# Layer 0 of a hybrid decoder trunk: the recurrent gate's projection as 512-wide products, and another order of work around the recurrence

## The chip, the cores and the metric

The kernel runs on one core of a Trainium2 chip. The metric is the device time of one execution in microseconds (us); below that stand profiled executions, in which the hardware recorded every instruction. The engines are named as in the profile: PE (TensorE, matrix products; PEld is its loading of stationary operands), DVE (VectorE), ACT (ScalarE), POOL (GpSimd) and SP (SyncE, which issues most DMAs).

## The reference

Two layers over x of 256 positions and width 1024, all in float32. Each layer normalizes x, projects it once into the inputs of three branches and their gates, and adds the projected, gated outputs to x:

```
proj = rms_norm(x) @ w_in        # a_q a_k a_v a_g | b_x b_g | c_q c_k c_v c_g
y_a = dilated_attention(a_q, a_k, a_v) * silu(a_g)      # 8 heads of 64
y_b = rg_lru(conv(b_x)) * silu(b_g)                     # width 256
y_c = stick_breaking_attention(c_q, c_k, c_v) * silu(c_g)   # 4 heads of 64
x = x + concat(y_a, y_b, y_c) @ w_out
```

The recurrent branch (b) is a linear recurrence h[t] = a[t] h[t-1] + u[t], with r and i two sigmoid gates of the convolved input xc, log a = 8 r log_sigmoid(lambda), and u = sqrt(1 - a^2) i xc. Its gate silu(b_g) multiplies h. A last normalization follows the two layers.

## The kernel before

**Precision.** PE multiplies in a reduced float32 format. So that nothing is lost, each weight and each activation is split into a rounded part (hi, made by ACT, line 115) and its rest (lo, made by DVE as the difference, line 117), and a product is the sum of hi*hi, hi*lo and lo*hi.

**Weights.** They come in chunks of 128 x 2048, two DMAs on SP each (line 108), into staging tiles st of which there are five. Each chunk is split in four parts of 512 columns, `rounds[l, c]` (ACT) and `rests[l, c]` (DVE), into tiles whi and wlo, of which there are four each; so chunk n + 4 can only be rounded when PE has read chunk n. In layer 0 the order of the chunks is CQ, CK, AQ0, AK0, BX, AQ1, AK1, CG, BG, AG, AG+1 and then four of the output projection, O to O+3 (called O1, O2, O3 here for O+1 to O+3). Chunk BG gives the recurrent gate, AG and AG+1 the gates of the attention heads, CG that of the stick-breaking heads. A chunk is requested one or two chunks ahead (`ask`).

**Projections** (`proj_b`, line 326). A chunk of 256 output columns is made in two halves of 128, with the weights stationary. There are two forms. A chunk that is not in PAIRED[l] takes 24 products of 256 columns a half, all into one PSUM bank for both halves (`mm3`, line 225): hi weights with the x's hi, hi weights with its lo, lo weights with its hi. A chunk in PAIRED[l] takes 8 products of 512 columns (line 344: hi weights with the x's hi and lo side by side) and 8 of 256 columns (line 341: lo weights with the x's hi) a half, into a bank of its own; first half hi weights first, second half lo weights first. ACT then copies the bank's right side into `low` (line 347), and DVE adds the left side to it (line 349). In layer 0 the result is still to be scaled by the row norms rb (`scaled`, line 415), since x goes in unnormalized there; then comes the sigmoid (line 439) and a multiplication (line 440).

**Order.** PE runs in the order of the program text (`manual_schedule`). The other engines' order is made when the program is built, by a list scheduler that takes what it reckons ready, earlier text first. `dep(a, b)` makes it place a behind b; in this diff both are always on one engine, so nothing is synchronized by it, and at run time each engine simply goes through its list.

**Around the change, layer 0.** PE's list is: CG; the transposes of the first four heads' probabilities; BG's first half; then `third()`: the recurrent gates (line 609), the values of the stick-breaking heads, those of the first four attention heads (line 458, into a bank of the pool pp), and the scores of the last four; BG's second half; AG; AG+1; and the output projection in the order of output tiles (t, n2) = (0,0), transposes of the last four heads, (1,0), (0,1), values of the last four heads, (1,1), each over the recurrent and stick-breaking part of y (chunks O and O1); then the attention part (O2, O3). The pool pp has three banks. The first attention values keep one from line 690 until `emit_y(y_c["y"], ...)`, line 715, has multiplied them (line 444); output tile (0,0) goes to another pool, the later ones to pp.

The recurrence (`lru_gates`, `lru_scan`) goes over ACT and DVE in turns: gates (ACT), `silu(bg)`: scaled (DVE), sigmoid (ACT), multiplication (DVE); a table load (line 78) on ACT, the decays av (line 623), a2 = av^2 (line 626, `last["a2"]`), the gap (a2 + 1) th (line 627), logarithm and exponential for its root (lines 628 and 629), products and the scan (lines 630 and 632), y = h * gate (line 444), its hi part (line 446) and its rest (line 447), which PE reads in output tile (0,0). In the same stretch runs the softmax of the last four heads (`dil_softmax`, line 560): eight exponentials (line 566, `last["exps"]`), four reciprocals (line 568, `last["recs"]`) and eight multiplications (line 570).

Of the kernel before, what the change touches and what calls it, by code (L numbers as in the profile page):

```python
# [12 lines left out]
AF = mybir.ActivationFunctionType  # L13
ALU = mybir.AluOpType
# [28 lines left out]

CH_AV, CH_CV, CH_CQ, CH_CK, CH_BX, CH_CG, CH_BG, CH_AG, CH_O = 0, 2, 3, 4, 7, 10, 11, 12, 14
CH_AQ, CH_AK = (5, 8), (6, 9)
PAIRED = ((CH_BX, CH_AQ[1], CH_AK[1], CH_CG, CH_AG, CH_AG + 1), (CH_CQ, CH_CK, CH_AQ[0], CH_AK[0], CH_BX, CH_AQ[1], CH_AK[1], CH_CG, CH_BG, CH_AG, CH_AG + 1))


@with_exitstack
def trunk_kernel(ctx: ExitStack, tc: tile.TileContext, x, first_x, first, wpack, prm_d, gatew, gains, consts, rope, out):  # L50
    nc = tc.nc
    act, dve, pe, gps = nc.scalar, nc.vector, nc.tensor, nc.gpsimd
# [10 lines left out]
    def bank(pool, tag):  # L63
        return pool.tile([P, 512], F32, name=tag, tag=tag)

    def scr(w):
        return wk.tile([P, 512], F32, name="scr", tag="scr", bufs=SCR)[:, 0:w]
# [3 lines left out]
    def dep(inst, on):  # L71
        tc.add_manual_dep(inst.ins, on.ins.name, nosync)
        return inst
# [9 lines left out]
    def tab(*a, **k):  # L83
        i = dep(act.activation(*a, **k), loaded["load"])  # L84
        loaded["users"].append(i)
        return i

    def v2(a, n=2):
        return a.rearrange("p (b t) -> p b t", b=n)
# [10 lines left out]
    split, rounds, rests = {}, {}, {}  # L100
# [23 lines left out]
    def ask(l, c, ahead=AHEAD):  # L124
        last = order.index((l, c)) + ahead
        while pending and order.index(pending[0]) <= last:
            i = pending.pop(0)
            ready[i] = load_chunk(*i)

    def weights(l, c, ahead=AHEAD):  # L130
        ask(l, c, ahead)
        return ready.pop((l, c))
# [87 lines left out]
    def mm3(ps, lhs, rhs, ks, first, last, skip=False):  # L220
        lh, ll = lhs
        rh, rl = rhs
        seq = [(a, b, k) for a, b in ((lh, rh), (lh, rl), (ll, rh)) for k in ks]
        for i, (a, b, k) in enumerate(seq):
            pe.matmul(ps, a(k), b(k), start=first and i == 0, stop=last and i == len(seq) - 1,  # L225
                      skip_group_check=skip)

    last = {}
# [82 lines left out]
    for l in range(L):  # L311
# [14 lines left out]
        def proj_b(c, mid=None, to=None, sc=1.0):  # L326
            pair = c in PAIRED[l]
            hi, lo = [a.rearrange("p (k c) -> p k c", c=256) for a in weights(l, c, AHEAD - 1 if mid else AHEAD)]
            if pair:
                flat = None if to is not None else scr(512)  # L330
                to = [v2(flat)[:, b, :] for b in range(2)] if to is None else to
            else:
                flat = bank(pp, "pp")
            for b in range(2):
                cs = slice(b * P, b * P + P)
                if pair:
                    ps = last["bank"] = bank(pp, "pp")
                    seq = [(b ^ i, k) for i in range(2) for k in range(NK)]
                    for i, (is_lo, k) in enumerate(seq):
                        if is_lo:  # L340
                            pe.matmul(ps[:, 0:S], lo[:, k, cs], xh[:, k, :], start=i == 0, stop=i == len(seq) - 1,  # L341
                                      skip_group_check=True)
                        else:
                            pe.matmul(ps, hi[:, k, cs], xx[:, k].rearrange("p h t -> p (h t)"), start=i == 0,  # L344
                                      stop=i == len(seq) - 1, skip_group_check=True)
                    low = wk.tile([P, S], F32, name="low", tag="low", bufs=2)
                    last["low"] = last["low", c, b] = act.activation(low, ps[:, S:2 * S], AF.Copy, scale=sc)  # L347
                    if sc == 1.0:
                        last["sum"] = last["sum", c, b] = dve.tensor_add(to[b], ps[:, 0:S], low)  # L349
                    else:  # L350
                        dve.scalar_tensor_tensor(to[b], ps[:, 0:S], sc, low, ALU.mult, ALU.add)
                else:
                    mm3(flat[:, b * 256:(b + 1) * 256], [lambda k, a=a: a[:, k, cs] for a in (hi, lo)],
                        [lambda k, a=a: a[:, k, :] for a in (xh, xl)], range(NK), b == 0, True, True)
                if b == 0 and mid:
                    mid()
                    ask(l, c)
            return flat

        def proj_to(dst, c, mid=None, sc=1.0):  # L360
            if c in PAIRED[l]:
                proj_b(c, mid, [dst[:, b, :] for b in range(2)], sc)
# [67 lines left out]
        def home(tile_):  # L430
            return [tile_[:, b, :] for b in range(2)] if l == 0 else None

        def silu(dst, ps):
            sg = v2(scr(512))
            src = dst if ps is None else v2(ps)
            if l == 0:
                ps, src = src, v2(scr(512))
                scaled(src, ps.rearrange("p b t -> p (b t)"))
            tab(sg, src, AF.Sigmoid)
            dve.tensor_mul(dst, src, sg)  # L440

        def emit_y(src, gate, k0, n):
            dst = v2(scr(n * S), n)
            dve.tensor_mul(dst, src, gate)
            yh, yl = [v[:, k0 % 4:k0 % 4 + n, :] for v in ys[k0 // 4]]
            act.activation(yh, dst, AF.Copy)
            last["rest", k0] = dve.tensor_sub(yl, dst, yh.bitcast(F32))

        def head(h):
# [58 lines left out]
        def rotated(c, tiles, h0, tag, mid=None):  # L508
            dst = tiles[h0] = sb.tile([P, 2, S], F32, name=tag, tag=tag)
            tab_ = rp0 if l == 0 else rp  # L510
            pair = c in PAIRED[l]
            if pair:
# [75 lines left out]
        th = sb.tile([P, 2, S], F32, name="th", tag="th")  # L588
        bg = sb.tile([P, 2, S], F32, name="bg", tag="bg")
# [29 lines left out]
        def lru_scan():  # L619
            av = sb.tile([P, 2, S], F32, name="av", tag="bxp")  # L620
            for b in range(2):
                o = 2 * l + b
                tab(av[:, b, :], rt[:, b, :], AF.Exp, scale=c8[:, o:o + 1])
            dve.tensor_mul(it, it, xc)
            a2 = v2(scr(512))
            last["a2"] = dve.tensor_mul(a2, av, av)
            dve.scalar_tensor_tensor(a2, a2, 1.0, th, ALU.add, ALU.mult)
            tab(th, a2, AF.Ln, bias=tiny)
            tab(th, th, AF.Exp, scale=0.5)
            dve.tensor_mul(it, it, th)  # L630
            for b in range(2):
                dve.tensor_tensor_scan(rt[:, b, :], av[:, b, :], it[:, b, :], 0.0, ALU.mult, ALU.add)
# [57 lines left out]
            y_c["y"] = values(va, pts, 0, bank(pp, "pp"))  # L690
            y_c["s"] = dil_scores(4)

        bg_ps = proj_b(CH_BG, third)
        if l == 0:
            for r in rests[l, CH_AG + 1]:
                dep(r, cg_scaled)
# [9 lines left out]
        ps = None  # L706
        if CH_AG in PAIRED[l]:
            agf = sb.tile([P, 2, S], F32, name="agf", tag="cg")
# [3 lines left out]
        ps = proj_b(CH_AG) if ps is None else ps  # L712
        table(SIGM)
        silu(ag[:, 0:2, :], ps)
        emit_y(y_c["y"], ag[:, 0:2, :], 4, 2)
        seeded = proj_b(CH_AG + 1)
        silu(ag[:, 2:4, :], seeded)
        if l == 0:
            for r in rests[l, CH_O][1:]:
                dep(r, bg_scaled)  # L720
            for r in rounds[l, CH_O + 1][2:]:
                dep(r, last["low", CH_AG, 0])
            dep(last["a2"], last["sum", CH_AG, 0])
            for r in rounds[l, CH_O][1:]:
                dep(r, last["gate"])
            for r in (*rests[l, CH_O][4:], *rests[l, CH_O + 1]):
                dep(r, last["sum", CH_AG, 0])
        if CH_AG + 1 in PAIRED[l]:
            seeded = last["bank"]
# [12 lines left out]
            act.activation(seed, xres[:, 1, 512 + LATE:1024], AF.Copy)  # L742
        for n2 in range(2):
            w = weights(l, CH_O + n2)
            for t in range(NT):
                if l > 0 and (t, n2) == (1, 1):
                    tail = [(bank(yp, "y")[:, 0:LATE], 0, LATE), (seed, LATE, 512)]
                    for ps, c0, c1 in tail[::-1]:
                        out_mm(ps, w, t, 0, range(4), c0 == 0, False, c0, c1, c0 > 0)
                    continue  # L750
                o_ps[t, n2] = bank(at, "s") if (t, n2) == (0, 0) else bank(pp, "pp")
                for ks in ((0, 1), (2, 3)):
                    out_mm(o_ps[t, n2], w, t, 0, ks, ks[0] == 0, False)
                if (t, n2) == (0, 0):
                    y_c["p"] = dil_transposes(4)
                if (t, n2) == (0, 1):
                    emit_y(values(va, y_c["p"], 4), ag[:, 2:4, :], 6, 2)
# [133 lines left out]
```

## Time and profile before

| | us |
|---|---|
| median of three runs | 245.64 |
| lowest, highest | 245.21, 245.93 |
| the profiled execution | 244.72 |
| its span, first to last instruction | 242.8 |
| PE, DVE, ACT busy in it | 236.1, 202.2, 177.2 |

Views of the profile give start and duration of instructions in us from the start of the span. Rows of the timeline can hold several instructions (x2); an engine's next instruction can start while the end of the last is still counted, so a step is best read from start to start. A bracket at the end is idle time of the engine, and what ended it. The chain of waits goes back from the last instruction to what released each one.

### The profile page before, as it was taken

The page shows a single profiled execution, that of the slowest core. Times are in us where ns is not written, and L with a number is a line of the kernel's source. Part 1 is how long each engine was busy: PE and PEld are TensorE (multiplying, and loading weights), DVE is VectorE, ACT ScalarE, POOL GpSimd, SP SyncE. Part 2 cuts the span into 40 slices and gives each one's busy share as a digit, 9 for nine tenths or more (in the row PEclk, how much of TensorE's full clock was granted, in tenths as well). Part 3 has the DMA queues.
Part 4 walks back from the last instruction along what each step waited for, and adds up shares of the span by engine and source line. Part 5 has one row for each costly group of instructions (what it writes and reads, how often), then busy time and mean ns, then how long its engine had stood idle before and what let it go on. Part 6 is the DMA issues. An engine that isn't in the chain of part 4 may idle for free.

```text
span 242.8 us, 4458 instructions
## 1 busy us (share of the span) xinstructions
PE 236.1 (97%) x1587; PEld 203.5 (84%) x1587; DVE 202.2 (83%) x488; ACT 177.2 (73%) x392; POOL 10.4 (4%) x43
## 2 busy tenths in 40 slices
PE   8999999999999999999999999999999999999991
PEld 4888999998888888778888888888888888887881
DVE  3885898999999989997793666999999986997362
ACT  3769977839958789994863775876579858997243
POOL 0017200002000000000000000000010000000000
PEclk9999999999999999999999999999999999999998
DMA  6999988455266753269457397505470772000022
GB/s 187 403 274 385 403 319 270 155 177 182 79 211 219 245 166 117 87 171 341 181 173 257 109 288 281 179 16 187 163 216 26 242 257 75 11 0 3 0 86 88
DMA packets 14037, 43.88 MB, mean 181 GB/s; under 512 B 1728, under 2 KB 3008, under 8 KB 14016
## 3 DMA queue, kind: packets, MB, share of 16 engines
q1 hardware_dynamic: 13248, 42.43, 51.9%
q0 software_dynamic: 192, 0.52, 0.9%
q10 hardware_dynamic: 576, 0.66, 0.8%
q8 instruction: 12, 0.20, 0.4%
q14 instruction: 9, 0.07, 0.1%
HBM read 42.03 MB, written 1.05 MB: 177 GB/s over the span
## 4 chain that ended last, share of the span: by engine, by line
PE 69%; DVE 24%; DMA 2%; ACT 2%; issue 1%; SPq 0%; DVEq 0%
PE pp L225 19%; PE pp L344 17%; PE pp L341 9%; PE s L225 8%; DVE wlo L117 7%; PE s L181 4%; PE pp L385 2%; PE s L494 2%; DMA st<-first 2%; PE pp L181 2%; PE y L458 2%; DVE scr L555 2%; DVE pr L570 2%; DVE sw L485 1%; PE y L225 1%; PE s L548 1%
## 5 line engine op out<-in xcount | busy, mean ns | idle before, releaser
L117 DVE TENSOR_TENSOR wlo<-st,whi 128x512 fp32r<-128x512 f32 x128 | 82.6, 688 | 7.1 <-ACT whi L115 6.5
L115 ACT ACTIVATE whi<-st 128x512 fp32r<-128x512 f32 x130 | 73.1, 628 | 11.3 <-DMA st<-w_pack 7.3
L344 PE MATMUL pp<-xx,whi 128*128 128x512 f32 x272 | 66.5, 393 | 0.0
L344 PEld LDWEIGHTS pp<-xx,whi 128*128 128x128 f32 x272 | 49.4, 188 | 9.7 <-DVE q L349 0.3
L341 PEld LDWEIGHTS pp<-xx,wlo 128*128 128x128 f32 x272 | 35.2, 191 | 2.1 <-ACT scr L84 0.3
L341 PE MATMUL pp<-xx,wlo 128*128 128x256 f32 x272 | 36.8, 285 | 0.0
L225 PE MATMUL pp<-xx,whi 128*128 128x256 f32 x160 | 21.1, 285 | 0.0
L225 PEld LDWEIGHTS pp<-xx,whi 128*128 128x128 f32 x160 | 19.8, 191 | 0.5 <-issue 0.3
L347 ACT ACTIVATE low<-pp 128x256 f32<-128x256 f32 x34 | 12.5, 373 | 10.4 <-PE pp L344 9.6
L78 ACT ACT_TABLE_LOAD x13 | 16.7, 1283 | 1.9 <-PEq L884 1.7
L84 ACT ACTIVATE pr<-scr,mn 128x128 f32<-128x128 f32 (+1 forms) x32 | 14.2, 446 | 3.9 <-DVE mn L555 3.9
L225 PE MATMUL pp<-whi,yh 128*128 128x512 f32 (+1 forms) x48 | 14.1, 382 | 0.0
L225 PE MATMUL pp<-wlo,yh 128*128 128x512 f32 (+1 forms) x48 | 13.6, 372 | 0.0
L225 PE MATMUL pp<-whi,yl 128*128 128x512 f32 (+1 forms) x48 | 13.6, 371 | 0.0
L225 PE MATMUL pp<-xx,wlo 128*128 128x256 f32 x80 | 11.2, 283 | 0.0
L225 PEld LDWEIGHTS pp<-xx,wlo 128*128 128x128 f32 x80 | 10.3, 192 | 0.0
L181 PE MATMUL s<-whi,xx 128*128 128x512 f32 (+1 forms) x36 | 10.1, 399 | 0.1
L225 PEld LDWEIGHTS pp<-whi,yl 128*128 128x128 f32 x48 | 8.6, 188 | 1.6
L225 PEld LDWEIGHTS pp<-wlo,yh 128*128 128x128 f32 x48 | 8.6, 188 | 1.6
L225 PEld LDWEIGHTS pp<-whi,yh 128*128 128x128 f32 x48 | 8.3, 188 | 1.6 <-issue 0.3
L555 DVE CUSTOM_DVE_ANT_0 scr<-s,con 128x128 f32<-128x128 f32 (+1 forms) x32 | 9.2, 353 | 0.0
L485 DVE TENSOR_TENSOR_SCAN sw<-scr,con 128x127 f32<-128x127 f32 (+1 forms) x16 | 8.0, 540 | 0.9 <-ACT scr L84 0.9
(193 smaller groups left out, 375.3 us busy)
## 6 DMA issues: line engine op xcount, KB each, us to landing
st<-w_pack SPq DMA_DIRECT2D x66, 512.0 KB, 4.8
st<-first SPq DMA_DIRECT2D x7, 512.0 KB, 5.9
xres<-x_in SPq DMA_DIRECT2D x4, 256.0 KB, 6.7
gw_t<-gate_w SPq DMA_DIRECT2D x2, 256.0 KB, 6.7
gn<-gains SPq DMA_DIRECT2D x2, 256.0 KB, 6.5
xs<-xc POOLq DMA_DIRECT2D x4, 128.0 KB, 3.3
gf<-gains SPq DMA_DIRECT2D x2, 256.0 KB, 6.1
out<-st ACTq DMA_DIRECT2D x2, 192.0 KB, 2.0
```

The source lines that it names most:

```text
L78: load = act.preload_act_table_set(name)
L84: i = dep(act.activation(*a, **k), loaded["load"])
L115: split[l, c] = act.activation(h, part, AF.Copy)
L117: rests.setdefault((l, c), []).append(dve.tensor_sub(r, part, h.bitcast(F32)))
L181: pe.matmul(ps[t][:, c0:c1], a[:, k, t * P:(t + 1) * P], b, start=k == 0 and all(m[0] is not ps for m in seq[:i]), stop=k == NK - 1 and al ...
L225: pe.matmul(ps, a(k), b(k), start=first and i == 0, stop=last and i == len(seq) - 1, skip_group_check=skip)
L341: pe.matmul(ps[:, 0:S], lo[:, k, cs], xh[:, k, :], start=i == 0, stop=i == len(seq) - 1, skip_group_check=True)
L344: pe.matmul(ps, hi[:, k, cs], xx[:, k].rearrange("p h t -> p (h t)"), start=i == 0, stop=i == len(seq) - 1, skip_group_check=True)
L347: last["low"] = last["low", c, b] = act.activation(low, ps[:, S:2 * S], AF.Copy, scale=sc)
L385: pe.matmul(cv_bk[t][:, 0:512 >> i], a[:, k, t * P:(t + 1) * P], cv_w[k // 4][:, k % 4, 0:2 - i].rearrange("p h c -> p (h c)"), start=i == ...
L485: dve.tensor_tensor_scan(w[:, lo:lo + n][:, ::-1], om[:, lo + 1:lo + 1 + n][:, ::-1], diag[:, 255 - n:255][:, ::-1], 0.0, ALU.mult, ALU.add)
L555: last["min"] = dve.tensor_tensor_reduce(xs[:, cs], sps[h][:, cs], nmask[:, cs], -0.125, 3e38, ALU.add, ALU.min, mn[:, t:t + 1])
```

## The change

Four things, all in layer 0:

1. BG joins PAIRED[0]: 16 products of 512 and 16 of 256 columns replace 48 of 256. Each half has its own bank, a copy (line 347) and a sum (line 349) into bg; the scaling by rb then reads bg.
2. Behind the gap step (line 627) are placed: the last rest of chunk O, all rests of O1, and the last three reciprocals of the softmax. Behind the root's exponential (line 629): the last four exponentials of the softmax.
3. Behind the sigmoid of the first attention gate (`ag_sig`): the last two roundings of O1 and all of O2. That sigmoid itself stands behind the hi part of the recurrent y (`last["high", 2]`).
4. Behind the multiplication of the first attention values (`last["y", 4]`, line 444): the last three rests of O1 and all of O2.

The rest of the diff records instructions under names.

```diff
-PAIRED = ((CH_BX, CH_AQ[1], CH_AK[1], CH_CG, CH_AG, CH_AG + 1), ...
+PAIRED = ((CH_BX, CH_AQ[1], CH_AK[1], CH_CG, CH_BG, CH_AG, CH_AG + 1), ...
...
-        bg_ps = proj_b(CH_BG, third)
+        bg_ps = proj_b(CH_BG, third, home(bg))
...
         silu(ag[:, 0:2, :], ps)
+        ag_sig = last["sig"]
...
             dep(last["a2"], last["sum", CH_AG, 0])
+            for r in (*rests[l, CH_O][3:], *rests[l, CH_O + 1], *last["recs"][1:]):
+                dep(r, last["gap"])
+            for r in last["exps"][4:]:
+                dep(r, last["root"])
+            for r in rounds[l, CH_O + 1][2:]:
+                dep(r, ag_sig)
+            for r in rests[l, CH_O + 1][1:]:
+                dep(r, last["y", 4])
+            dep(ag_sig, last["high", 2])
             for r in rounds[l, CH_O][1:]:
                 dep(r, last["gate"])
-            for r in (*rests[l, CH_O][4:], *rests[l, CH_O + 1]):
+            for r in (*rests[l, CH_O][3:], *rests[l, CH_O + 1]):
                 dep(r, last["sum", CH_AG, 0])
...
             w = weights(l, CH_O + n2)
+            if l == 0 and n2 == 0:
+                for r in rounds[l, CH_O + 2]:
+                    dep(r, ag_sig)
+                for r in rests[l, CH_O + 2]:
+                    dep(r, last["y", 4])
```

`home(bg)` gives the two halves of bg as targets in layer 0 and nothing in layer 1, where BG was in PAIRED already.

More of the change, by code (lines that the diff above doesn't have):

```diff
@@ L45 @@
 CH_AQ, CH_AK = (5, 8), (6, 9)
-PAIRED = ((CH_BX, CH_AQ[1], CH_AK[1], CH_CG, CH_AG, CH_AG + 1), (CH_CQ, CH_CK, CH_AQ[0], CH_AK[0], CH_BX, CH_AQ[1], CH_AK[1], CH_CG, CH_BG, CH_AG, CH_AG + 1))
+PAIRED = ((CH_BX, CH_AQ[1], CH_AK[1], CH_CG, CH_BG, CH_AG, CH_AG + 1), (CH_CQ, CH_CK, CH_AQ[0], CH_AK[0], CH_BX, CH_AQ[1], CH_AK[1], CH_CG, CH_BG, CH_AG, CH_AG + 1))
 @with_exitstack
@@ L438, in silu @@
                 scaled(src, ps.rearrange("p b t -> p (b t)"))
-            tab(sg, src, AF.Sigmoid)
+            last["sig"] = tab(sg, src, AF.Sigmoid)
             dve.tensor_mul(dst, src, sg)
@@ L443, in emit_y @@
             dst = v2(scr(n * S), n)
-            dve.tensor_mul(dst, src, gate)
+            last["y", k0] = dve.tensor_mul(dst, src, gate)
             yh, yl = [v[:, k0 % 4:k0 % 4 + n, :] for v in ys[k0 // 4]]
-            act.activation(yh, dst, AF.Copy)
+            last["high", k0] = act.activation(yh, dst, AF.Copy)
             last["rest", k0] = dve.tensor_sub(yl, dst, yh.bitcast(F32))
@@ L626, in lru_scan @@
             last["a2"] = dve.tensor_mul(a2, av, av)
-            dve.scalar_tensor_tensor(a2, a2, 1.0, th, ALU.add, ALU.mult)
+            last["gap"] = dve.scalar_tensor_tensor(a2, a2, 1.0, th, ALU.add, ALU.mult)
             tab(th, a2, AF.Ln, bias=tiny)
-            tab(th, th, AF.Exp, scale=0.5)
+            last["root"] = tab(th, th, AF.Exp, scale=0.5)
             dve.tensor_mul(it, it, th)
```

## The prediction

> **What bounds the kernel now.** I read the page first, then the waits of TensorE between 22 and 238 us, then its timeline around the change, and last the timelines of VectorE and ScalarE in the same stretch.
>
> ```profile
> span 242.8 us, 4458 instructions
> PE 236.1 (97%) x1587; PEld 203.5 (84%) x1587; DVE 202.2 (83%) x488; ACT 177.2 (73%) x392; POOL 10.4 (4%) x43
> ```
> ```profile
> PE s L225 <- DVE yl L447: 0.2, 1, 0.2
> ```
>
> The second fence is the whole answer for TensorE's waits: one, on line 447, the rest of the gated recurrence output. A busy PE is no proof that it is never held, so I looked at the starts of its matmuls.
>
> ```profile
> 81.92 2.17 PE L225 MATMUL pp<-xx,whi 128*128 128x256 f32 x16
> 83.93 1.12 PE L225 MATMUL pp<-xx,wlo 128*128 128x256 f32 x8
> 84.89 2.00 PE L344 MATMUL pp<-xx,whi 128*128 128x512 f32 x8
> ...
> 88.64 3.82 PE L344 MATMUL pp<-xx,whi 128*128 128x512 f32 x16
> 92.30 2.08 PE L341 MATMUL pp<-xx,wlo 128*128 128x256 f32 x16
> ...
> 97.86 0.61 PE L225 MATMUL s<-wlo,yh 128*128 128x512 f32 x2
> 98.65 0.73 PE L225 MATMUL s<-whi,yl 128*128 128x512 f32 x2 [0.17 <-DVE yl L447]
> 99.22 1.48 PE L494 MATMUL s<-con,pr 128*128 128x128 f32 x12
> 100.46 0.73 PE L225 MATMUL pp<-whi,yh 128*128 128x512 f32 x2
> ```
>
> From 81.92 to 97.86 one group starts where the former leaves off. Sixteen 512-wide products take 92.30 - 88.64 = 3.66, so a pair takes 0.46. The pair at 97.86 holds the engine for 98.65 - 97.86 = 0.79, and the pair after it, started from rest, 99.22 - 98.65 = 0.57: 0.33 of waiting and 0.11 of starting again, 0.44 us together. That is all that TensorE loses in the stretch that the change touches.
>
> Next to it stands a second limit that no list of waits shows. The products at 100.46 (output tile t = 1, n2 = 0) need a bank of the pool pp, which has three. One holds the first attention group's result until line 444 multiplies it by its gate; the others hold the two halves of the last projection until line 349 sums them.
>
> ```profile
> 84.56 0.69 DVE L447 TENSOR_TENSOR yl<-scr,yh 128x512 fp32r<-128x512 f32 x1
> 85.16 0.69 DVE L415 SCALAR_TENSOR_TENSOR scr<-pp,rb 128x512 f32<-128x512 f32 x1
> ...
> 89.04 0.42 DVE L349 TENSOR_TENSOR agf<-pp,low 128x256 f32<-128x256 f32 x1 [0.79 <-ACT low L347]
> ...
> 92.19 0.67 DVE L117 TENSOR_TENSOR wlo<-st,whi 128x512 fp32r<-128x512 f32 x1
> ...
> 97.31 0.69 DVE L117 TENSOR_TENSOR wlo<-st,whi 128x512 fp32r<-128x512 f32 x1
> 97.91 0.69 DVE L447 TENSOR_TENSOR yl<-scr,yh 128x512 fp32r<-128x512 f32 x1
> ...
> 99.11 0.69 DVE L117 TENSOR_TENSOR wlo<-st,whi 128x512 fp32r<-128x512 f32 x1
> 99.71 0.69 DVE L444 TENSOR_TENSOR scr<-pp,ag 128x512 f32<-128x512 f32 x1
> 100.31 0.75 DVE L349 TENSOR_TENSOR scr<-pp,low 128x256 f32<-128x256 f32 x2
> 100.97 0.69 DVE L117 TENSOR_TENSOR wlo<-st,whi 128x512 fp32r<-128x512 f32 x1
> ```
> ```profile
> 215.00 1.48 PE L494 MATMUL s<-con,pr 128*128 128x128 f32 x12
> 216.24 0.70 PE L225 MATMUL pp<-whi,yh 128*128 128x512 f32 x2
> ```
> ```profile
> 89.00:100.40 11.40, 11.23 (x63) 9.41 (x62) 11.36 (x29) 11.21 (x32) 0.00 (x0) 1.00 0.33 109
> ```
>
> The multiplication ends at 99.71 + 0.69 = 100.40, the sums later still, so the bank at 100.46 is the multiplication's, freed 0.06 before. TensorE was not held there: the step from the transposes takes 100.46 - 99.22 = 1.24, as the same step in layer 1 does (216.24 - 215.00), where nothing presses. But there is no slack: had TensorE come earlier, it would have waited. So two clocks run to the same point. VectorE has no idle time between 89.04 and 100.31 (11.36 busy of 11.40 in the last fence, third busy figure). A gain for TensorE is kept only as far as VectorE reaches line 444 earlier.
>
> **The change, part by part.**
>
> *The gate's products.* The 48 products of 256 columns of chunk BG become 16 of 512 and 16 of 256 (the same columns in all).
>
> ```profile
> 31.39 5.75 PE pp L225 x48
> ...
> 143.43 3.65 PE pp L344 x16
> 147.09 1.91 PE pp L341 x16
> ```
>
> These rows of the chain of waits price both: 5.75 before, 3.65 + 1.91 = 5.56 after; gain 0.19, all of it on TensorE's path. [...]
>
> *The new sums.* Each half now needs a copy on ScalarE (line 347) and a sum on VectorE (line 349); two sums occupy 100.97 - 100.31 = 0.66, so 0.33 each. The scaling by rb (line 415) stays, from SBUF instead of PSUM; no row shows this one, but at 0.69 it is as long as other 512-wide operations here, so I take no difference. The first sum falls into a stretch in which VectorE is full, and pushes line 447 from 84.56 to 84.89. The second half's products end at about 84.86 (84.89 less 0.19, and the last of a group ends 0.16 after the next group's start: 88.64 + 3.82 against 92.30). Its copy (0.36 at 88.65, below) is done by about 85.3, below the 85.49 at which VectorE is free. So the scaling moves from 85.16 to 85.16 + 0.66 = 85.82, and everything chained to it on ScalarE moves by the same 0.66:
>
> ```profile
> 84.13 1.15 ACT L115 ACTIVATE whi<-st 128x512 fp32r<-128x512 f32 x2 [1.12 <-PE pp L225]
> 85.88 0.64 ACT L84 ACTIVATE scr<-scr 128x512 f32<-128x512 f32 x1 [0.60 <-DVE scr L415]
> 86.54 1.28 ACT L78 ACT_TABLE_LOAD   x1
> ...
> 88.65 0.36 ACT L347 ACTIVATE low<-pp 128x256 f32<-128x256 f32 x1
> ```
>
> Sigmoid, table load, two decays, the copy at 88.65, and the sum at 89.04, which comes to 89.70. Bounds: 0.33, if VectorE drops a split to make room for the first sum; upwards, the rival below.
>
> *The order on VectorE.* Counting instructions of line 117 four to a chunk, the splits at 92.19, 97.31 and 99.11 are those of the second, third and fourth parts of chunk O1; they now stand behind line 444. That takes three splits at 0.60 (97.91 - 97.31) out of the way, 1.80. The last split of chunk O, done before 89.04 so far, now stands behind the gap step (line 627) and comes in: 0.60. So line 444's multiplication, with VectorE full throughout, gives way to the next at 100.31 + 0.66 - 1.80 + 0.60 = 99.77, 0.54 earlier than before. If the first split of O1, free to come at any time after the gap step, also slips behind it, 1.14 earlier.
>
> *The order for line 447.* It is the wait that shows. TensorE, 0.19 earlier and without its wait, wants the result at 97.86 + 0.46 - 0.19 = 98.13. Taking out the split at 97.31 alone puts its end at 98.00. The other reorderings (the later exponentials behind the root, the reciprocals behind the gap step) take further work out of its way, against the 0.66. I cost this wait at nothing afterwards; if that is wrong, up to 0.44 comes back.
>
> *The rest.* Roundings and rests of chunk O2 and most of O1 move behind the attention gate's sigmoid and line 444. TensorE reads O1 only after twelve 512-wide products from 100.46, 2.75 later, and its three moved splits take 1.80. Their staging buffers are released later, and with them SP's next weight transfers, which serve chunks past 110 us; I cost that at nothing. The last projection's sums now stand behind three splits and one rest, 99.77 + 4 x 0.60 + 0.33 = 102.50, and must free a bank by 100.46 + 2.75 - 0.54 = 102.67: enough, barely.
>
> *Sum.* TensorE alone: 0.19 + 0.44 = 0.63 off. VectorE at line 444: 0.54 off (up to 1.14, and less by the rivals). The smaller one counts: about 0.5. One more check: the projection's third half starts at 88.64 + 8 x 0.229 = 90.47, now 90.28, in the bank that the sum of 89.04 frees, now at 89.70 + 0.42 = 90.12, plus 0.06: 0.10 of slack. The profiled execution took 244.72 (span 242.8) and becomes 244.2; the runs' median is 245.64, 0.92 above it, so I predict 245.1. A measurement of this kernel can tell about 0.3%, 0.74 us, from no change; the gain stays below it.
>
> **The rivals.**
>
> *The slack is eaten (no gain).* Three places have 0.1 or less to spare: the bank at 90.28, line 444 and the bank at 102.67. If the order puts 0.5 more in front of any of them, the gain is gone: 245.4 to 246.0. For it: VectorE takes on 0.66 and three limits lie together. Against it: the three splits taken out are certain.
>
> *The roundings stand in front of the copy (slower).* In before the two roundings at 84.13 waited 1.12 for TensorE to have read the first-half weights of BG, which it had at 83.93, when it turned to wlo. The new second half reads whi last, so they are free only at 84.86, the very time at which the copy of line 347 is. If they stand ahead of it in ScalarE's order, the chain is late by their 1.1 more: line 444 gives way at 100.87, 0.56 later than before, TensorE stands still in front of it, and the run takes 246.2. It decides from the point at which the sum of 89.04 comes after 90.3. Against it: the copy comes earlier in the program. [...]
>
> *More than TensorE's 0.63.* If VectorE is ahead everywhere and TensorE sets the end: 245.0. Further gain has no source here, as TensorE has no other wait to lose.
>
> *Nothing comes of the order.* If the reorderings leave line 444 behind the same work, the sums alone cost 0.66: 246.3.
>
> **How the numbers follow.** Forecast, 0.4 to 0.63 off: 0.55. Slack eaten: 0.24. Roundings in front: 0.12. Order without effect: 0.05; a gain for a reason not seen: 0.04. The range leaves some 0.3 on either side of the cases for the median of a few runs (245.21 to 245.93 before): 244.6 to 246.1. Faster by over 0.3% would be below 244.9; the forecast lies 0.2 short of it, so a part of its chance falls there: 0.28. Slower by over 0.3% would be above 246.38; half of the two upper cases, and a little for a stall longer than I priced: 0.12. Within: 0.60.
>
> **What would show it.** Right: L344 x16 and L341 x16 where L225 stood at 74 and 82 us; the wait on line 447 gone; the sum of 89.04 near 89.7; line 444's third execution near 99.2, and TensorE's products at 100.46 near 99.9. Wrong: a wait of TensorE at L344 near 90.3 (bank), a start after 100.46 of the second output tile, a new wait of TensorE past 102 us, or ScalarE's L115 ahead of L347 near 85.

## The result, and the profile after

The changed kernel took 246.81 us (median of 6 runs, 246.43 to 247.56) against 245.52 for the kernel before (6 runs, 245.21 to 245.93): a ratio of 1.0056, 95% interval 1.0039 to 1.0072. I had predicted 245.1, in a range of 244.6 to 246.1. It is slower, and outside the range.

Two later comparisons of the same two kernels, with 12 runs each of the changed one, gave 1.0018 (1.0003 to 1.0032) and 1.0020 (1.0003 to 1.0037), with before at 244.63 and 244.56. So the loss is there in all three, and its size in two of them is 0.2%, about 0.5 us; the rest of the first figure did not come back (more on this at the experiments).

The page of the profiled execution after (246.43 us, 1.71 longer than the one before):

```profile
span 244.5 us, 4427 instructions
PE 237.6 (97%) x1571; PEld 202.8 (83%) x1571; DVE 202.9 (83%) x490; ACT 177.6 (73%) x394; POOL 10.6 (4%) x43
```

The two sums show as 490 DVE instructions for 488, the two copies as 394 ACT instructions for 392, the wide products as 16 fewer of PE. The waits of PE between 22 and 238 us, where before had one row, are an empty list:

```profile
engine line waited for: us in total, times, longest us
```

A list of waits that is empty, and a longer run: so the time must be found in the starts. These are PE's in before that the prediction did not show:

```profile
5.80 0.66 PE L181 MATMUL s<-whi,xx 128*128 128x256 f32 x4
...
28.12 2.08 PE L225 MATMUL pp<-xx,whi 128*128 128x256 f32 x16
...
72.50 1.48 PE L494 MATMUL s<-con,pr 128*128 128x128 f32 x12
...
111.77 0.61 PE L225 MATMUL s<-whi,yh 128*128 128x512 f32 x2
...
119.93 1.04 PE L273 MATMUL s<-con,scr 128*128 128x128 f32 x8
...
127.63 1.04 PE L273 MATMUL s<-con,scr 128*128 128x128 f32 x8
128.42 1.17 PE L385 MATMUL pp<-whi,xx 128*128 128x512 f32 x4
```

And the same places after:

```profile
6.05 1.05 PE L181 MATMUL s<-whi,xx 128*128 128x256 f32 x4
...
28.89 2.30 PE L225 MATMUL pp<-xx,whi 128*128 128x256 f32 x16
...
73.50 1.48 PE L494 MATMUL s<-con,pr 128*128 128x128 f32 x12
...
89.47 4.05 PE L344 MATMUL pp<-xx,whi 128*128 128x512 f32 x16
93.35 2.08 PE L341 MATMUL pp<-xx,wlo 128*128 128x256 f32 x16
...
99.87 1.48 PE L494 MATMUL s<-con,pr 128*128 128x128 f32 x12
101.19 0.73 PE L225 MATMUL pp<-whi,yh 128*128 128x512 f32 x2
...
112.58 0.69 PE L225 MATMUL s<-whi,yh 128*128 128x512 f32 x2
...
121.08 1.29 PE L273 MATMUL s<-con,scr 128*128 128x128 f32 x8
...
129.09 1.21 PE L273 MATMUL s<-con,scr 128*128 128x128 f32 x8
130.06 1.17 PE L385 MATMUL pp<-whi,xx 128*128 128x512 f32 x4
```

Take the difference of the two starts, place by place. At the transposes ahead of the change (72.50 and 73.50) PE is already 1.00 late, and all engines have had the same instructions in the same order up to there. That 1.00 belongs to the execution, not to the change, and I take it off everywhere ("net"):

- 88.64 to 89.47: 0.83, net -0.17. The wide products' gain.
- 92.30 to 93.35: 1.05, net +0.05. The row at 89.47 lasts 4.05, where the one of 88.64 before lasts 3.82: PE lost about 0.2 at its bank, waiting and starting again, too short to stand in the list of waits.
- 99.22 to 99.87: net -0.35. The wait on line 447 is gone.
- 100.46 to 101.19: net -0.27. Output tile (1,0), held by its bank, 0.08.
- 111.77 to 112.58: net -0.19, then the row after it net -0.11; the hi part of the last y came late (line 446 at 111.88 for 108.92, net 1.96 later).
- 119.93 to 121.08, net +0.15; the row lasts 1.29 for 1.04, so by its end net +0.4.
- 128.42 to 130.06: net +0.64, and this stays to the end.

Up to 101 us the change gains 0.27. From there to 130 us it loses 0.91. DVE and ACT after, with the rows that belong to those places:

```profile
79.13 0.42 DVE L349 TENSOR_TENSOR bg<-pp,low 128x256 f32<-128x256 f32 x1
79.56 0.69 DVE L440 TENSOR_TENSOR cg<-scr 128x512 f32<-128x512 f32 x1
...
83.17 0.68 DVE L117 TENSOR_TENSOR wlo<-st,whi 128x512 fp32r<-128x512 f32 x1
...
86.60 0.41 DVE L349 TENSOR_TENSOR bg<-pp,low 128x256 f32<-128x256 f32 x1
87.05 0.69 DVE L415 SCALAR_TENSOR_TENSOR scr<-bg,rb 128x512 f32<-128x512 f32 x1
...
90.93 0.42 DVE L349 TENSOR_TENSOR agf<-pp,low 128x256 f32<-128x256 f32 x1 [1.39 <-ACT low L347]
...
100.44 0.69 DVE L444 TENSOR_TENSOR scr<-pp,ag 128x512 f32<-128x512 f32 x1
...
112.52 0.69 DVE L447 TENSOR_TENSOR yl<-scr,yh 128x512 fp32r<-128x512 f32 x1 [0.40 <-ACT yh L446]
...
115.06 2.50 DVE L117 TENSOR_TENSOR wlo<-st,whi 128x512 fp32r<-128x512 f32 x4 [0.64 <-ACT whi L115]
117.47 0.68 DVE L796 TENSOR_TENSOR xres<-s,xres 128x512 f32<-128x512 f32 x1
```
```profile
85.94 0.38 ACT L347 ACTIVATE low<-pp 128x256 f32<-128x256 f32 x1 [2.09 <-PE pp L344]
86.22 1.15 ACT L115 ACTIVATE whi<-st 128x512 fp32r<-128x512 f32 x2
...
110.82 1.16 ACT L115 ACTIVATE whi<-st 128x512 fp32r<-128x512 f32 x2 [1.24 <-DMA st<-w_pack]
111.88 0.61 ACT L446 ACTIVATE yh<-scr 128x512 fp32r<-128x512 f32 x1
114.39 2.33 ACT L115 ACTIVATE whi<-st 128x512 fp32r<-128x512 f32 x4 [1.90 <-DMA st<-w_pack]
```

The first attention sum, at 89.04 before, is at 90.93: net 0.89 later, where I had 0.66. Line 444 is at 100.44 for 99.71: net 0.27 earlier, where I had 0.54. And past 110 us ACT stands before roundings that wait for their transfer (1.24, 1.90), with the last y's hi part (line 446) and, on DVE, the residual add (line 796) queued behind them. Before, they stood behind the same roundings; but the pair ahead of the hi part, the last two of the six at 105.26, was done in time:

```profile
105.26 3.24 ACT L115 ACTIVATE whi<-st 128x512 fp32r<-128x512 f32 x6
108.92 0.63 ACT L446 ACTIVATE yh<-scr 128x512 fp32r<-128x512 f32 x1 [0.43 <-DVE scr L444]
111.13 1.16 ACT L115 ACTIVATE whi<-st 128x512 fp32r<-128x512 f32 x2 [1.57 <-DMA st<-w_pack]
```

That pair rounds the second half of layer 1's first chunk. By the traces its transfer was issued at 103.53 and landed at 107.28 before; after, it is issued at net 105.07 and lands at net 109.80. This goes with the new orders: the transfer lands at net 107.05 to 108.23 in the four profiles without them (before, e1, e2, e7), and at 108.83 to 109.98 in the ten with them.

### The profile page after: what moved, and what is told of

It is laid out like the page before. It is cut to its first block, busy times and chain, and to the rows that moved or that the text cites. A ratio compares the mean times of both kernels' runs of the same rounds, so it can differ in the third digit from the quotient of the medians.

```text
span 244.5 us, 4427 instructions
## 1 busy us (share of the span) xinstructions
PE 237.6 (97%) x1571; PEld 202.8 (83%) x1571; DVE 202.9 (83%) x490; ACT 177.6 (73%) x394; POOL 10.6 (4%) x43
## 3 DMA queue, kind: packets, MB, share of 16 engines
HBM read 42.03 MB, written 1.05 MB: 176 GB/s over the span
## 4 chain that ended last, share of the span: by engine, by line
PE 94%; DMA 2%; DVE 1%; SPq 0%; issue 0%; ACT 0%; DVEq 0%
PE pp L344 27%; PE pp L225 22%; PE pp L341 14%; PE s L225 9%; PE s L181 4%; PE s L494 3%; DMA st<-first 2%; PE y L458 2%; PE pp L385 2%; PE s L548 2%; PE pp L181 2%; PE s L474 1%; PE y L225 1%; PE pp L458 1%; PE s L273 1%; PE s L609 1%
## 5 line engine op out<-in xcount | busy, mean ns | idle before, releaser
L344 PE MATMUL pp<-xx,whi 128*128 128x512 f32 x288 | 70.6, 393 | 0.0
L344 PEld LDWEIGHTS pp<-xx,whi 128*128 128x128 f32 x288 | 52.3, 188 | 10.6 <-DVE agf L349 0.5
L341 PEld LDWEIGHTS pp<-xx,wlo 128*128 128x128 f32 x288 | 37.3, 191 | 2.3 <-ACT scr L84 0.3
L347 ACT ACTIVATE low<-pp 128x256 f32<-128x256 f32 x36 | 13.3, 374 | 12.5 <-PE pp L344 11.7
L225 PE MATMUL pp<-xx,whi 128*128 128x256 f32 x128 | 17.0, 284 | 0.0
L225 PEld LDWEIGHTS pp<-xx,whi 128*128 128x128 f32 x128 | 16.0, 191 | 0.5 <-issue 0.3
L181 PE MATMUL s<-whi,xx 128*128 128x512 f32 (+1 forms) x36 | 10.6, 413 | 0.3 <-DVE whi L163 0.2
L570 DVE TENSOR_SCALAR pr<-pr,den 128x128 f32<-128x128 f32 (+1 forms) x32 | 8.5, 313 | 0.1
L181 PEld LDWEIGHTS s<-whi,xx 128*128 128x128 f32 x36 | 6.7, 218 | 2.1 <-ACT xx L161 0.8
```

What stands on the lines that cost most here:

```text
L181: pe.matmul(ps[t][:, c0:c1], a[:, k, t * P:(t + 1) * P], b, start=k == 0 and all(m[0] is not ps for m in seq[:i]), stop=k == NK - 1 and al ...
L570: dve.tensor_scalar(pr[:, cs], pr[:, cs], den[:, t:t + 1], None, ALU.mult)
```

## The experiments

The theories, with the letters by which some expectations name them. **S**: the loss is the gate's two copies and sums, which delay the chain through ACT and DVE. **A**: the loss is a steady one at the turn of the layers, from the weight splits that the new order leaves in front of the residual add. **E**: that loss belongs to the transfers of one execution. **F**: the offset at the start belongs to the execution as well, whatever the kernel. Each row below is read like the list above: the shift at the transposes of 72.50, and, net of it, the shift of output tile (1,0) (100.46 in before), of the products at 117 us (ahead of the turn of the layers), and of the first products past it (128.42).

| kernel | ratio to before (95%) | shift at 72.50 | net 100.46 | net 117 | net 128.42 |
|---|---|---|---|---|---|
| after | 1.0056 (1.0039 to 1.0072) | +1.00 | -0.27 | -0.08 | +0.64 |
| e1 before again | 1.0005 (0.9987 to 1.0022) | -0.50 | -0.02 | +0.01 | +0.01 |
| e2 gate alone | 1.0044 (1.0027 to 1.0061) | +0.44 | +0.90 | +0.93 | +0.93 |
| e3 orders alone | 0.9975 (0.9963 to 0.9987) | +0.23 | -0.44 | -0.43 | -0.43 |
| e4 without part 4 | 1.0018 (1.0002 to 1.0033) | -0.18 | +0.51 | +0.54 | +0.54 |
| e5 after again | 1.0018 (1.0003 to 1.0032) | +0.28 | -0.35 | -0.03 | +0.20 |
| e6 after, turn freed | 1.0015 (0.9999 to 1.0031) | +0.66 | -0.35 | +0.10 | +0.10 |
| e7 sums, narrow products | 1.0039 (1.0021 to 1.0057) | +0.99 | +1.19 | +1.19 | +1.19 |
| e8 orders, turn freed | 0.9985 (0.9969 to 1.0000) | -0.66 | -0.44 | -0.43 | -0.43 |
| e9 first split behind | 1.0007 (0.9987 to 1.0027) | +0.71 | -0.50 | -0.19 | -0.12 |
| e10 O2 free | 1.0015 (1.0001 to 1.0029) | -0.09 | +0.20 | +0.31 | +0.30 |
| e11 after, third time | 1.0020 (1.0003 to 1.0037) | +1.15 | -0.36 | +0.02 | +0.02 |
| e12 last hi part first | 0.9997 (0.9977 to 1.0016) | -0.45 | -0.51 | -0.42 | -0.24 |

The ratios come from 6 to 12 executions, the shifts from one each: a ratio says how much, a shift where.

**e1: the kernel before, unchanged.** 

> The kernel before, once more, for a second profile of it. All theories: a ratio of 1.00 to the kernel before, 245.3 to 245.9 us. The profiled execution of the changed kernel was already 0.8 us later than that of before at 7.4 us, when nothing of the change has run, and 1.0 later at 30 us. Theory F (the start of an execution varies by about 1 us, whatever the kernel): this profile's products at line 181 reach 7.4 us of before anywhere between 7.4 and 8.2. Rival (the changed program starts slower): they stand at 7.4 again, within 0.1.

Measured: 244.79 us, ratio 1.0005. Its profiled execution is 0.50 ahead of the first profile at 72.50 and stays there. Its products of 7.38 start at 6.66, earlier than either theory had them. So a half microsecond of start comes and goes with the kernel unchanged, as F says; the 1.00 of after needs no effect of the change, though one profile each can't exclude a small one.

**e2: the gate's products and sums alone.**

```diff
-PAIRED = ((CH_BX, CH_AQ[1], CH_AK[1], CH_CG, CH_AG, CH_AG + 1), ...
+PAIRED = ((CH_BX, CH_AQ[1], CH_AK[1], CH_CG, CH_BG, CH_AG, CH_AG + 1), ...
-        bg_ps = proj_b(CH_BG, third)
+        bg_ps = proj_b(CH_BG, third, home(bg))
```

> The kernel before with the 512-wide gate products alone, none of the new orders. Theory A (staging tiles held): the two new sums push VectorE's chain by 0.66 us, so the waits at lines 447 and 444 come 0.5 to 0.7 later while nothing holds the staging tiles: 245.9 to 246.2 us (ratio 1.001 to 1.003), and TensorE does not wait at the transposes of line 273 before layer 1. Rival B (the gate's new sums and banks are the whole loss): 246.6 to 246.9, as the changed kernel. Rival C (the new products are a gain by themselves, 0.19): 245.3.

Measured: 246.04 us, ratio 1.0044, the largest loss among the experiments, above A's range. The waits of PE:

```profile
PE s L225 <- DVE yl L447: 0.4, 1, 0.4
PE s L225 <- ACT yh L446: 0.3, 1, 0.3
```

The wait on line 447 has grown and has a second one ahead of it, on the hi part of the same y. PE's shift goes from -0.17 after the gate's products to +0.90. Net of the start, the gate's scaling (line 415) is 0.91 later than in before, line 447 is 0.91 later, and PE behind it 0.90 to 0.93: the delay that the two sums make goes through the chain whole.

**e3: the orders alone** (after, with BG taken out of PAIRED[0]). 

> The changed kernel with the gate's products in the old form, 48 of 256 columns: the new orders alone. Theory A: line 444 comes about 1.2 earlier, TensorE loses its 0.44 at line 447, but the weight transfers from chunk O3 on are issued 1.5 to 8 us later than before, and TensorE waits 0.3 to 0.6 at line 273: 245.4 to 245.9 us in all (ratio 0.999 to 1.002). Rival B: the orders are a pure gain, 245.0 (ratio 0.998). Rival D (the orders are the whole loss): 246.5 and more.

Measured: 244.32 us, ratio 0.9975 (0.9963 to 0.9987): a gain. PE and DVE:

```profile
72.73 1.48 PE L494 MATMUL s<-con,pr 128*128 128x128 f32 x12
...
100.25 0.70 PE L225 MATMUL pp<-whi,yh 128*128 128x512 f32 x2
```
```profile
98.79 0.69 DVE L444 TENSOR_TENSOR scr<-pp,ag 128x512 f32<-128x512 f32 x1
```

Line 444 is net 1.15 earlier (98.79 - 99.71 - 0.23), PE is rid of the 0.44 at line 447, loses nothing elsewhere, and keeps the gain to the end: rival B, not A, which had a loss at line 273.

**e4: after without its fourth part** (rests of O1 and O2 no longer behind line 444).

```diff
-            for r in rests[l, CH_O + 1][1:]:
-                dep(r, last["y", 4])
...
-                for r in rests[l, CH_O + 2]:
-                    dep(r, last["y", 4])
```

> The changed kernel without its fourth part: the rests of chunks O1 and O2 need not stand behind line 444; all else as in the changed kernel. Only one split moves on VectorE, from behind line 444 to just ahead of it. Theory A: the transfers of O3 and layer 1 are issued earlier, if only as much as this one split gives, and part of the 0.5 at line 273 goes: 246.3 to 246.6 us. Rival B: no change, 246.8, or worse by the split ahead of line 444 (up to 0.6, 247.2).

Measured: 245.18 us, ratio 1.0018, beside e2 and e3. In its profile PE loses 0.58 at the bank of line 444 (net -0.08 to +0.50), which comes net 0.52 later than before, where after has it 0.27 earlier. One split (0.60) stands in front of it again; another 0.3 of the difference is there already at the gate's scaling (net 86.35, for 86.05 in after). So the fourth part does at line 444 what it is for; the time is no worse without it than with it (1.0018 in e5).

**e5: after, unchanged.** 

> The changed kernel once more, beside the others of this call. Its first profile, set against one of before at the same place ahead of the change, loses 0.19 us at the bank of the attention gate's projection, 0.09 at the bank of line 444, and 0.73 at the turn to layer 1 (the two sets of transposes at line 273); gains are 0.16 and 0.40. Theory A (the layer turn is a steady loss, made by the held staging tiles): 0.5 to 0.7 at line 273 again, ratio 1.004 to 1.006. Rival E (it hangs on the transfers' times of that execution): 0.3 or less at line 273, ratio 1.002 to 1.003, as for the kernel with the free rests.

Measured: 245.16 us, ratio 1.0018. Up to 101 us its profile repeats the first one of after within 0.1; past it, 0.55 is lost instead of 0.91. The loss at the turn is 0.23 instead of 0.72: E's figure, not A's.

**e6: after, with the splits of layer 1's second chunk behind the residual adds.**

```diff
-                dve.tensor_add(xres[:, t, cs], o_ps[t, n2], xres[:, t, cs])
+                add = dve.tensor_add(xres[:, t, cs], o_ps[t, n2], xres[:, t, cs])
+                if l == 0 and t == 0:
+                    for r in rests[1, CH_AV + 1][2 * n2:2 * n2 + 2]:
+                        dep(r, add)
```

> The changed kernel, with the four rests of layer 1's second chunk placed behind the additions to the residual (two behind the first, two behind the second) that they stood in front of. Theory A: the normed x is ready before TensorE asks for it, no wait at line 273, 0.5 to 0.7 us better than the changed kernel (ratio 1.001 to 1.003). Rival E: no better than the changed kernel in the same call, within 0.2. If these rests are needed earlier by layer 1 than they then come: a new wait of TensorE at the first products of layer 1.

Measured: 245.10 us, ratio 1.0015. Its profile loses nothing at the turn (net +0.10 ahead of it and past it), yet the time is that of e5. A falls as the cause of the steady loss: freeing the turn is not worth 0.7.

**e7: the copies and sums with the old, narrow products.**

```diff
+                elif to is not None:
+                    ps = bank(pp, "pp")[:, 0:S]
...
+                    low = wk.tile([P, S], F32, name="low", tag="low", bufs=2)
+                    act.activation(low, ps, AF.Copy, scale=0.5)
+                    dve.scalar_tensor_tensor(to[b], ps, 0.5, low, ALU.mult, ALU.add)
```

Each half has its own bank, as in the change; the copy takes half of it and the sum adds the other half, so that the result is the same. The sum is a fused operation here, of the same 0.42 us as the change's.

> The kernel before with the gate's products in their old form, 48 of 256 columns, but each half in a bank of its own, with a copy on ScalarE (of half the value) and a sum on VectorE (half the value and the copy) as in the changed kernel. Theory S (the copy and the sum are the loss of the gate's part): 0.1 to 0.2 worse than the wide products alone, ratio 1.005 to 1.0055 (246.1 us where before has 244.84). Rival W (the wide products themselves lose, by their order of weights or their banks): ratio 1.000 to 1.002.

Measured: 245.37 us, ratio 1.0039 (1.0021 to 1.0057), which can't be told from e2's 1.0044. The waits of PE are e2's too (this kernel's line 454 is 447 there, 453 is 446):

```profile
PE s L225 <- DVE yl L454: 0.4, 1, 0.4
PE s L225 <- ACT yh L453: 0.3, 1, 0.3
```

S holds: the copies and sums make the loss. Here too the delay goes through whole: the scaling (line 422 there), line 454 and PE are each net 1.19 later than in before. The second bank came along in this kernel, so e7 alone doesn't part it from the sums; PE does lose 0.39 at a bank by 92.30, but its two listed waits are for the chain. What the wide products give back (0.17 in the profiles) is too little to see in the time.

**e8: the orders alone, with e6's edit.** 

> The new orders alone, with the old products, and the rests of layer 1's second chunk behind the residual additions as well. It is to be the fastest version. Theory A: the turn has 0.2 to 0.4 us to spare in the profile of the orders alone, so no gain over it in the median: ratio 0.997 to 0.998. If the turn costs something in many executions: 0.996.

Measured: 244.12 us, ratio 0.9985 (0.9969 to 1.0000), beside e3's 0.9975. Where the sums are absent nothing is late at the turn (net -0.43 ahead of it and past it in both), and the edit is worth nothing.

**e9: after, with O's first split behind the gate's scaling.** In after that split (83.17) stands ahead of the score minima, in front of the chain. It did so in before too, a little earlier in the list (the last of the three at 79.33):

```profile
79.33 1.89 DVE L117 TENSOR_TENSOR wlo<-st,whi 128x512 fp32r<-128x512 f32 x3
```

```diff
-            for r in rests[l, CH_O][1:]:
+            for r in rests[l, CH_O]:
                 dep(r, bg_scaled)
```

> After, with the first rest split of chunk O (line 117), which stands ahead of the score minima there (83.17 in the profile after), held behind the gate's scaling (line 415), where VectorE idles later on (1.39 us ahead of the sum of agf). If the chain through the gate's sums is what line 444 waits for, the sum of agf comes 0.35 to 0.6 earlier net of the start (net of it +0.2 to +0.5 against before, where after has +0.8 to +0.9), line 444 is 0.3 to 0.6 earlier, TensorE's waits at the bank of chunk AG+1 and of line 444 (0.09 to 0.19 each) go, and the run is 0.3 to 0.5 us below after's own in this call: ratio to before 0.997 to 1.000. If the chain is not what decides and the late waits come from the transfers alone, the ratio is after's own, 1.002 to 1.005, and the profile shows the earlier sum with the waits past 104 us as large as in after.

Measured: 244.81 us, ratio 1.0007 (0.9987 to 1.0027), beside 1.0020 for after in the same comparison; the intervals overlap. DVE's chain:

```profile
86.07 0.42 DVE L349 TENSOR_TENSOR bg<-pp,low 128x256 f32<-128x256 f32 x1 [0.40 <-ACT low L347]
86.53 0.69 DVE L415 SCALAR_TENSOR_TENSOR scr<-bg,rb 128x512 f32<-128x512 f32 x1
...
90.41 0.42 DVE L349 TENSOR_TENSOR agf<-pp,low 128x256 f32<-128x256 f32 x1 [0.78 <-ACT low L347]
...
99.92 0.69 DVE L444 TENSOR_TENSOR scr<-pp,ag 128x512 f32<-128x512 f32 x1
```

The split out of the way is worth 0.1 to 0.2 on the chain (e11's attention sum is net 0.79 later than before, this one 0.66) and not the 0.35 to 0.6 I expected, since DVE now waits 0.40 for the copy: net of 0.71 the scaling is at 85.82 and the attention sum at 89.70, line 444 0.50 earlier than before. PE's offset at 100.46 improves from -0.36 (e11) to -0.50; past it, 0.38 is still lost. The time lies between the two ranges that I gave.

**e10: after, with the roundings and rests of O2 not held.**

```diff
-            if l == 0 and n2 == 0:
-                for r in rounds[l, CH_O + 2]:
-                    dep(r, ag_sig)
-                for r in rests[l, CH_O + 2]:
-                    dep(r, last["y", 4])
```

> After without the last clause of the fourth part and of the third that concerns chunk O2: its roundings are no longer held behind ag_sig, nor its rests behind line 444, so the staging buffers come free earlier. If the held buffers cause the waits past 104 us (0.52 net in the second profile of after, 0.88 in the first), SP's issue of the second half of O3 moves from 101.8 back towards 93 to 98, these waits go, and the ratio is 0.3 to 0.6 us below after's own. If they come from the late chain, or change from one execution to the next, the issue moves and the ratio stays at after's own, or rises by up to 0.6 us, because one or two splits come back in front of line 444.

Measured: 245.08 us, ratio 1.0015. SP issues the second half of O3 no earlier (101.18, for 101.85 in e11, with starts 1.24 apart, so net 0.57 later), against my expectation; that of layer 1's first chunk comes at 104.25 for 106.12, net 0.63 earlier, but lands no earlier (net 109.95, for 109.87). The losses past 104 us go (0.1 in all), and PE has a wait for line 444:

```profile
PE pp L225 <- DVE scr L444: 0.2, 1, 0.2
```

The losses do not go because the work was set free. The last y's hi part starts at net 111.03 (110.95 in e11), the first step of the next norm at the turn (line 207) at net 116.61 (116.53): as late as in e11. PE, held at line 444, comes 0.56 later than there (net +0.20 for -0.36), and so finds them ready. What the held buffers cost past 104 us, e10 doesn't show.

**e11: after, unchanged, for the third time.** 

> The changed kernel once more, unchanged, beside the two above. Two comparisons gave 1.0056 and 1.0018, with intervals that do not meet. If the first six executions were off as a set, this one gives 1.001 to 1.003; if the effect is really half a per cent and the second comparison was off, 1.004 to 1.007.

Measured: 245.12 us, ratio 1.0020. It agrees with e5 and not with the first comparison, in which before too was 0.7 to 1.0 above its later medians. What made those first executions of after longer by another 0.8 us, beside before in the same comparison, was not found: the one profile of them has 0.4 of it more than e5's past 101 us (transfers that land later, at the turn) and a start that is 0.72 later.

**e12: e9, with the last y's hi part in front of the roundings that wait for their transfer.** On ACT alone, line 446 changes places with two roundings.

```diff
+        if l == 0:
+            for r in rounds[1, CH_AV][2:]:
+                dep(r, last["high", 6])
```

> The kernel with O's first split behind the gate's scaling, and besides the rounding of the last y (line 446, k0 = 6) put ahead of the two roundings of the second half of layer 1's first chunk, which stand in front of it in ScalarE's queue and wait for their transfer (1.24 us in the profile after, 1.33 in the one with the split behind). If TensorE's loss between 111 and 114 us (0.21 to 0.35 in the profiles of the changed kernel) comes from that place in the queue, it goes: the offset of TensorE's products stays within 0.05 from 111.5 to 113.5, and the end is 0.1 to 0.3 earlier net of the start than with the split alone (net -0.13 there), unless the layer turn takes it back. If it comes from VectorE's splits in front of line 444 (five in a row at 107.23), or from the transfers themselves, the loss stays, and the time is that of the split alone: ratio 0.999 to 1.002.

Measured: 244.73 us, ratio 0.9997 (0.9977 to 1.0016). Its DVE (chain) and ACT:

```profile
89.25 0.42 DVE L349 TENSOR_TENSOR agf<-pp,low 128x256 f32<-128x256 f32 x1 [0.78 <-ACT low L347]
...
98.76 0.69 DVE L444 TENSOR_TENSOR scr<-pp,ag 128x512 f32<-128x512 f32 x1
```
```profile
109.17 0.63 ACT L446 ACTIVATE yh<-scr 128x512 fp32r<-128x512 f32 x1 [1.32 <-DVE scr L444]
109.71 1.14 ACT L115 ACTIVATE whi<-st 128x512 fp32r<-128x512 f32 x2
```

The hi part no longer stands behind a transfer, and PE's shift does not move by 0.05 between 104 and 127 us, where e9 lost 0.2 at 112. That place in ACT's queue was the cause of that loss. 0.18 at the second half of the turn remains. With both repairs the whole change comes out even with before; the orders without the gate's sums (e3) beat both kernels.

## Why the prediction was wrong, step by step

*The gate's products.* Predicted 0.19 off PE (a 512-wide product at 3.66 / 16 = 0.229, a 256-wide one at 5.75 / 48 = 0.120 in before); 0.17 measured. Right.

*The new sums.* Predicted: the scaling at 85.82, the first attention sum at 89.70, so 0.66 later. Measured net: 86.05 and 89.93 in after (0.89 later than before; 0.80 in e5, 0.79 in e11). The path of the chain was right, the price of its sums too low. I took 0.33 a sum from two sums back to back, neither of which reads the other. The second sum here is followed by the scaling that reads it, 0.45 later (86.60 to 87.05). The first costs 0.34 in e5 and e11, and 0.43 in after (79.13 to 79.56), where the multiplication behind it comes 0.09 later; its sigmoid stands behind the new copy on ACT. The kernel before had the right price in one place: two sums and the scaling of their result, 76.92 - 76.12 = 0.80:

```profile
76.12 0.76 DVE L349 TENSOR_TENSOR cg<-pp,low 128x256 f32<-128x256 f32 x2
76.92 0.69 DVE L415 SCALAR_TENSOR_TENSOR scr<-cg,rb 128x512 f32<-128x512 f32 x1
```

That e9 has exactly 85.82 and 89.70 is luck: a split is gone from in front of the chain there, a wait of 0.40 for the copy has come, and the second sum costs 0.46.

*The order at line 444.* Predicted 0.54 earlier. Measured 0.27 in after, 0.35 in e5, 0.36 in e11 (line 444 itself, and PE behind it), 0.50 in e9, and 1.15 in e3. The mechanism is right; the size is off by the price of the sums (0.23 in after, 0.13 to 0.14 in e5 and e11), and by a memset (line 593, 0.08) that the scheduler now puts directly in front of line 444.

*The order for line 447.* Right in every kernel that has it: the wait is gone.

*The bank at 90.28.* I gave it 0.10 of slack; with the chain 0.2 later than I had it, PE loses 0.2 there (4.05 for 3.82): 0.10 of waiting, until the sum ends at 90.93 + 0.42 = 91.35 and the next weight load starts at 91.41, and 0.11 of starting again. It loses 0.14 in e5 and e11, and nothing in e9. That is the rival "the slack is eaten", in its first place; at its second, the bank of line 444, PE loses 0.08 to 0.11 in after, e5 and e11.

*The step that failed* is in "The rest": the held roundings and rests release their "staging buffers ... later, and with them SP's next weight transfers, which serve chunks past 110 us; I cost that at nothing". Past 101 us after gives back 0.91, e5 0.55, e11 0.38, where I had nothing. The transfers do come later (net 109.80 for 107.28, above). e12 shows one part of what that costs: a rounding of layer 1 that waits for its transfer stood in front of the last y on ACT. Another is the turn of the layers, 0.72 in the first profile, 0.23 in the second, 0 in the third. It takes both parts of the change. The orders alone (e3) hold the same buffers and lose nothing: without the sums the transfer is issued 0.9 earlier than in after and lands 0.6 earlier (net 109.20), and the hi part starts at net 110.28 instead of 110.88. The gate alone (e2, e7) loses nothing there; PE is late by then itself. With that, "the smaller one counts: about 0.5" could not hold either: what PE gained by 101 us was not the end's to keep.

*The rivals.* Roundings in front of the copy: no, line 347 runs at 85.94, line 115 behind it at 86.22. Nothing comes of the order: no, e3 gains 0.25%. More than PE's 0.63: no. The price that I put in the fourth rival on the sums alone, 0.66, was too low: e2 and e7 are slower by 1.1 and 1.0 us (1.0044 and 1.0039 of 244.84 and 244.63), 0.93 and 1.19 in their profiles.

Roughly, then, by the ratios: the orders give 0.6 us (e3), the sums cost 1.1 (e2), and together they cost the 0.5 of e5 and e11. That it adds up so well is partly chance: place by place the two don't add, for the waits that make nearly all of e2's loss are gone in after, and what after loses it loses elsewhere.

The later medians of after, 245.16 and 245.12, lie on the 245.1 that I forecast. That is luck too: the kernel before stood 1 us lower there than the 245.64 I counted from, and the change went the other way.

*What stays open.* Why the first six executions of after were another 0.8 us longer. Whether the medians of the kernels with the sums (e5, e6, e11: 0.5 us above before) hold more than their profiles show (0.02 to 0.20): with one profile each this can't be told from the scatter of the start. One rival is left here: the shift at 72.50 is +0.45 on average over the ten profiles with the sums and -0.23 over the four without, with a scatter of about 0.5 in each group, so that a program with the sums may start a little later; no run settles it. A larger number of staging tiles was not tried.

## What to carry to other kernels

Two copies and two sums on a chain through three engines cost more here (1.1 us in e2) than PE gained by sixteen products fewer (0.17): price an edit by what queues behind it, take the price from a row in which the same instruction follows (0.80 from the start of two sums to that of the scaling, where I had 0.66 for the two), and test the edit and the reordering that is to pay for it apart, since one can hide the other. Holding work back to clear a stretch sends it somewhere: look for what then stands behind it in each engine's queue, above all behind an instruction that waits for a transfer (1.33 us on ACT in e9, with the last y's hi part behind it, and 0.2 lost by PE). And before two traces are compared, take off the shift that they already have ahead of the first changed instruction (1.00 here).

## What the runs showed of the hardware

The start of an execution differs by 1.8 us (shift at 72.50 from -0.66 to +1.15) among the fourteen profiles, before's and the table's, in which every engine has the same order of instructions up to there. Part of it is PE's pace in its first microseconds: the four 256-wide products at 5.80 in before are 0.12 apart (the next group starts at 6.30), the four at 6.05 after are 0.22 apart (next at 6.91), and only those at 7.27 are 0.12 apart there. Before has the slower pace too, but only up to 5.80: its pair at 5.37 is 0.22 apart. The granted clock in the profile does not show the change of pace, at 1.00 from 4.0 to 7.5 us in both; what sets the moment at which it comes was not shown. Another part is transfers: for those of four roundings (line 115) ACT waits 1.36 and 0.78 us in after (rows at 18.98 and 20.91), 1.04 in before (18.32). The roundings at 27.14 in before come at 28.54 after, PE's weight load waits 0.17 for a rounding at 29.74, and the group at 28.89 takes 2.30 for 2.08. In e11 PE waits 0.24 for a rounding in the same group.

From a sum to the instruction that reads its result DVE took 0.45 (86.60 to 87.05; 0.46 in e9), where two sums that don't read each other took 0.33 each (100.97 - 100.31 = 0.66 in before). And PE lost time behind a wait as well: behind the hold at 98.65 in before the next pair took 0.57 for 0.46, and the same 0.11 stands behind the shorter hold (0.10) at the bank in after.

The list of waits shows less than the starts do: the hold at line 447 in before is 0.33 by the starts and 0.17 in its bracket, since the end of the former pair is still counted; the 0.2 at 89.47 and those at 112 and 121 us are seen only in a row that lasts longer than its like.
